# Two-layer trunk on one core: the scan's table copies and the second half's first operands placed behind the loop over channel tiles

## The chip, the cores and the metric

The kernel runs on one core of a Trainium2 chip. The metric is the device time of one execution in microseconds (us); a measurement gives the median of several runs. The engines are named as the profile names them: PE (TensorE, matmul), PEld (its weight loads), DVE (VectorE), ACT (ScalarE), POOL (GpSimd) and SP (SyncE, which issues the DMAs).

## The reference

Two layers of a trunk are computed for two groups of tokens that share their weights: 128 context tokens and 512 tokens that are being denoised, each of width 1024, held together as 640 columns. The part that matters here is the beginning of a layer:

```
mod = silu(c) @ w_ada[l] + b_ada[l]
sh1, sc1, g1, sh2, sc2, g2 = split(mod, 6)
u = x * (1.0 + sc1) + sh1
z = u @ w_in
q, k, v, s_in, f_in, gates = split(z)
...
ssm_y, ssm_state = s5_bidirectional(s_in, a_re, a_im, log_dt, b_re, b_im, c_re, c_im, d, h0)
```

The modulation `mod` comes from the condition vector alone. `u` is the modulated input and the operand of the large product `z`, of which `s_in` feeds a bidirectional state-space scan. The scan's coefficients (powers of exp(a dt), and from them the zero-order-hold input matrices) are computed on the chip from `a_re`, `a_im` and `log_dt`. Attention, a Fourier branch, gating, the output product, a layer norm and a convolution-gated MLP follow; the change does not touch them.

## The kernel before

The 640 columns are worked on in two halves: half 0 has 256 columns (the 128 context tokens and 128 others), half 1 has 384. The 1024 channels are eight tiles of 128, numbered `dt` or `kt`. Products run in split precision: a number is stored as a rounded part h (a cast on ACT, line 113) and the remainder l (a subtraction, line 114, on DVE unless another engine is named), and each tile of a product takes three matmuls, h·h, h·l and l·h (lines 131 to 133, or 1359 in the first loop).

The program begins in `run` (line 1318 on). `silu_c` makes the condition's operand `cs`. `ssm_scalars` (line 463 on) computes, on DVE, the powers `PW` of the scan's coefficient and the table `FB`; eight copies on ACT (lines 568, 569, 571 and 572) then bring them into the layouts `LT` and `FTab`, in one go for both layers (`G` = 64 groups) and separately for the forward partitions 0 to 63 and the backward ones 64 to 127, with the order of the eight time steps turned round in one of the two. The copy writes with the time step as the fastest index of its target and reads with the group as the fastest of its source. Line 573 adds a table with the sign turned.

`ada_first` (line 238) is the first loop: for each of the eight channel tiles it loads a block `ablk` of 1 MB, makes scale and shift of that tile (`adps` on PE, copied to `adar` on ACT, turned round on PE as `adpt`, added up on DVE as `mod`) and calls `block(dt)`. `block` makes the operands of the input product for that channel tile with `modsplit` (line 366): it scales and shifts the input `xs` into a buffer `ut` (two buffers, line 369), on ACT or, for the tiles listed in `MOD0`, on POOL; then it casts `ut` into `uh` on ACT and subtracts into `ul` on DVE. Half 0 is made tile by tile in the loop. Half 1 is made for tiles 0 to 5 when `dt` is `XB` = 5, and tile by tile after that; `MOD0` gives POOL the tiles 1, 3, 5 and 7 of half 1.

While the loop runs, PE already works on the first four weight tiles of the input product for half 0. `WAT` = (3, 6, 7, 7) says at which `dt` each of the four is loaded and begun, with all channel tiles up to there; every later `dt` adds its three matmuls to each open tile. The four sums stay in four PSUM banks (`mm_first`) until the copy `sre` on ACT (line 776) empties them. The products of half 1 over the same tiles (`mm_wz`, lines 131 to 133) take the next bank that comes free.

After the loop, `ssm_prep(0, ...)` makes the scan's matrices for layer 0, eight chunks of them, on DVE and POOL by turns (its first instruction is `nci`, line 617; `pt`, `bb`, `wbt`, `pb` and `wct` are its tiles; it reads `FTab` and `LT`), with transposes (`ptp`) and small products (`pkp`) on PE; and `shift` subtracts the mean of the input (`shs`, `mm_shift`, `xs`). Both are held behind the last subtraction of either half by `behind` (line 95), which lets a scheduler place instructions only after a given one. The layer's scan reads tables (`wbd`, `pd`) that prep has written through DMAs; `Ms` is loaded from `pd`.

The order of instructions on each engine is not written by hand: a scheduler sets it when the program is built, from the order of the code, `behind` and its own estimates. Each engine then works its list off in order, and a waiting instruction holds all behind it.

## Time and profile before

| what | us |
|---|---|
| median of 3 runs | 2289.36 |
| the runs | 2283.41, 2289.46, 2289.36 |
| the profiled execution's own time | 2281.54 |
| its span in the trace | 2279.4 |

The profile shows one execution. Busy time of an engine is the union of its instructions' durations; a row of the timeline gives the start, the duration (of all instructions merged into it) and, in brackets, the idle time of the engine ahead of it and what ended it. Windows give the busy time of each engine in a stretch, the TensorE clock that was granted (1.00 is 2.4 GHz, 0.50 is 1.2 GHz), the share of the DMA engines and the rate of transfers.

### The profile page before, as it was taken

To read this page: it belongs to the slowest core of one execution; us is meant where nothing else is said; L and a number is where in the kernel's file an instruction comes from. 1 tells how busy PE (TensorE), PEld (TensorE's weight loads), DVE (VectorE), ACT (ScalarE), POOL (GpSimd) and SP (SyncE) were. 2 spreads that over 40 slices of the span, in tenths; PEclk is the share of its full clock that TensorE was granted. 3 is DMA by queue.
4 is the path that set the end of the run, shared out by engine and by line. 5 is a ranking of instruction groups with operands and counts; after the bars stand their busy time and mean duration, and the time that the engine had idled before them with its cause. 6 is when DMAs were issued, how large, how long until landed. Compare 5 with 4: busy or idle time off the path is not lost.

```text
span 2279.4 us, 40654 instructions
## 1 busy us (share of the span) xinstructions
PE 2201.7 (97%) x15696; PEld 2114.2 (93%) x15696; DVE 1517.7 (67%) x3638; ACT 879.0 (39%) x1799; POOL 598.5 (26%) x589
## 2 busy tenths in 40 slices
PE   6899999999999999999998999999999999999997
PEld 5889989898799999999998999999879999999997
DVE  7956750466757788999974277357755776475475
ACT  5343232344633441431444322334553443242243
POOL 0439952007354300000035000002535520000003
PEclk8999989999999999999999999999999999999998
DMA  7786575625032135445436745542204122222221
GB/s 277 215 259 213 205 214 168 213 89 165 2 128 82 58 110 167 140 142 184 146 93 174 178 130 146 159 158 78 76 2 153 57 82 67 84 75 65 84 75 47
DMA packets 172641, 293.97 MB, mean 129 GB/s; under 512 B 48128, under 2 KB 114080, under 8 KB 171424
## 3 DMA queue, kind: packets, MB, share of 16 engines
q1 hardware_dynamic: 171584, 291.12, 41.8%
q8 instruction: 124, 2.03, 0.4%
q14 instruction: 69, 0.57, 0.1%
q10 hardware_dynamic: 864, 0.26, 0.1%
HBM read 241.57 MB, written 49.75 MB: 128 GB/s over the span
## 4 chain that ended last, share of the span: by engine, by line
PE 78%; DVE 10%; DMA 6%; ACT 2%; POOL 2%; issue 1%; SPq 1%; POOLq 0%; DVEq 0%; ACTq 0%
PE mm_w_up L133 7%; PE mm_w_up L131 7%; PE mm_w_up L132 7%; PE mm_wz L131 6%; PE mm_wz L132 6%; PE mm_wz L133 6%; PE mm_qkv L1108 4%; PE mm_w_down L131 4%; PE mm_w_down L133 4%; PE mm_w_down L132 4%; DVE adjunk L283 2%; PE mm_pv L1173 2%; PE pt L1226 2%; PE S L1215 2%; PE mm_w_br L131 2%; PE mm_w_br L132 2%
## 5 line engine op out<-in xcount | busy, mean ns | idle before, releaser
L113 ACT CAST wh<-wraw 128x1024 fp32r<-128x1024 f32 (+1 forms) x224 | 232.7, 1039 | 426.4 <-PE mm_w_down L132 118.6
L132 PE MATMUL mm_w_up<-ul,wh 128*128 128x256 f32 (+1 forms) x1280 | 393.9, 309 | 0.0
L133 PE MATMUL mm_w_up<-uh,wl 128*128 128x256 f32 (+1 forms) x1280 | 393.4, 309 | 0.2 <-POOL wl L114 0.2
L131 PE MATMUL mm_w_up<-uh,wh 128*128 128x256 f32 (+1 forms) x1280 | 392.3, 309 | 1.2 <-ACT wh L113 0.8
L114 POOL TENSOR_TENSOR wl<-wraw,wh 128x1024 fp32r<-128x1024 f32 x64 | 157.0, 2454 | 871.6 <-ACT wh L113 854.0
L114 DVE TENSOR_TENSOR wl<-wraw,wh 128x1024 fp32r<-128x1024 f32 (+1 forms) x160 | 203.4, 1271 | 148.7 <-ACT wh L113 146.0
L131 PE MATMUL mm_wz<-uh,wh 128*128 128x384 f32 (+1 forms) x832 | 264.9, 319 | 6.2 <-ACT uh L113 3.2
L1252 DVE SCALAR_TENSOR_TENSOR acc<-mm_w_up,cw,acc 128x127 f32<-128x127 f32 (+2 forms) x616 | 228.5, 398 | 53.9 <-ACT acc L1258 32.7
L132 PE MATMUL mm_wz<-ul,wh 128*128 128x384 f32 (+1 forms) x832 | 261.7, 315 | 2.7 <-DVE ul L114 2.7
L133 PE MATMUL mm_wz<-uh,wl 128*128 128x384 f32 (+1 forms) x832 | 261.8, 315 | 0.0
L131 PEld LDWEIGHTS mm_w_up<-uh,wh 128*128 128x128 f32 x1280 | 241.9, 189 | 1.6 <-ACT wh L113 1.0
L133 PEld LDWEIGHTS mm_w_up<-uh,wl 128*128 128x128 f32 x1280 | 242.2, 189 | 0.6 <-POOL wl L114 0.5
L132 PEld LDWEIGHTS mm_w_up<-ul,wh 128*128 128x128 f32 x1280 | 242.3, 189 | 0.3
L133 PE MATMUL mm_w_down<-hh,wl 128*128 128x256 f32 (+1 forms) x632 | 195.0, 310 | 0.9 <-DVE wl L114 0.9
L132 PE MATMUL mm_w_down<-hh,wh 128*128 128x384 f32 (+1 forms) x632 | 195.5, 310 | 0.0
L131 PE MATMUL mm_w_down<-hh,wh 128*128 128x384 f32 (+1 forms) x632 | 193.5, 311 | 0.0
L131 PEld LDWEIGHTS mm_wz<-uh,wh 128*128 128x128 f32 x832 | 159.2, 191 | 15.0 <-issue 6.3
L132 PEld LDWEIGHTS mm_wz<-ul,wh 128*128 128x128 f32 x832 | 159.4, 192 | 3.8 <-DVE ul L114 3.0
L133 PEld LDWEIGHTS mm_wz<-uh,wl 128*128 128x128 f32 x832 | 159.4, 192 | 1.0 <-issue 1.0
L283 DVE SCALAR_TENSOR_TENSOR adjunk<-araw,cb 128x512 f32<-128x512 f32 x192 | 140.6, 732 | 12.1 <-DMA araw<-in_w_ada_t_dram 8.9
L1258 ACT ACTIVATE acc<-mm_w_up,cw 128x256 f32<-128x256 f32 (+1 forms) x176 | 107.4, 613 | 54.8 <-PE mm_w_up L133 53.3
L133 PEld LDWEIGHTS mm_w_down<-hh,wl 128*128 128x128 f32 x632 | 119.1, 189 | 1.5 <-DVE wl L114 1.5
(464 smaller groups left out, 5257.0 us busy)
## 6 DMA issues: line engine op xcount, KB each, us to landing
wraw<-in_w_up_dram SPq DMA_DIRECT2D x88, 512.0 KB, 3.5
wraw<-in_wz_dram SPq DMA_DIRECT2D x64, 512.0 KB, 3.9
araw<-in_w_ada_t_dram SPq DMA_DIRECT2D x48, 512.0 KB, 3.7
araw<-in_w_ada_dram SPq DMA_DIRECT2D x32, 512.0 KB, 4.2
wraw<-in_w_down_dram SPq DMA_DIRECT2D x32, 512.0 KB, 3.5
wraw<-in_w_br_dram SPq DMA_DIRECT2D x24, 512.0 KB, 3.7
td<-gt SPq DMA_DIRECT2D x48, 192.0 KB, 2.2
tl<-td SPq DMA_DIRECT2D x48, 192.0 KB, 3.4
```

What stands on the lines that cost most here:

```text
L113: nc.scalar.copy(h, src)
L114: return (eng or nc.vector).tensor_tensor(l, src, h.bitcast(F32), OP.subtract)
L131: mm(ps, wh, xh, start=j == 0, stop=False)
L132: mm(ps, wh, xl, start=False, stop=False)
L133: mm(ps, wl, xh, start=False, stop=j == n - 1)
L283: nc.vector.scalar_tensor_tensor(junk[:, :k.stop - k.start], raw[:, d], 1.0, cb[v], OP.mult, OP.mult, accum_out=part[:, c, vec - a, dt + d ...
L1108: nc.tensor.matmul(ps[:, :256], lt, w[:, c0:c0 + 256], start=k == 0, stop=k == 23)
L1173: nc.tensor.matmul(po[64 * hh:64 * hh + 64, :256], vt[:, kt + 1, kv * 64:kv * 64 + 64], PT[hh][:, kt], start=kt == 0, stop=kt == 5, tile_p ...
L1215: nc.tensor.matmul(S[:, b, :384], q, kt[:, hl, P + b * 384:P + (b + 1) * 384], start=hl == 0, stop=hl == 1)
L1226: nc.tensor.transpose(pt[:, j * P:(j + 1) * P], p[:, (3 * b + j) * P:(3 * b + j + 1) * P], self.ident)
L1252: nc.vector.scalar_tensor_tensor(o, src, w, o, OP.mult, OP.add)
L1258: nc.scalar.activation(acc, ps, AF.Identity, bias=b, scale=w1)
```

## The change

The eight copies of the tables leave `ssm_scalars` and become a function `ssm_tables(l)` of its own, called once for each layer after the loop, behind the last cast of half 0 (`cast0`): sixteen copies, each for the 32 groups of one layer. The sign copy is made for each layer, too. The pool `zoh` that holds `PW` and `FB` stays open until then. Half 1's operands are no longer made in the loop at `dt` 5, 6 and 7 but all eight tiles after the last `dt`, and POOL scales all eight (`MOD0`). `WAT` begins the second of the four first weight tiles at `dt` 5 and the third at 6.

```diff
-WAT = (3, 6, 7, 7)
-MOD0 = (((), ()), ((1, 3, 5, 7), ()))
+WAT = (3, 5, 6, 7)
+MOD0 = (((), ()), (range(8), ()))
...
     def split(self, h, l, src, eng=None):
         nc = self.nc
-        nc.scalar.copy(h, src)
+        self.cast = nc.scalar.copy(h, src)
...
-            fw, bw = slice(0, 64), slice(64, 128)
-            for ri in range(2):
-                o = self.LT[:, ri].rearrange("p g t -> p t g")
-                cp = nc.scalar.copy
-                cp(o[fw], PW[fw, ri, 1:9])
-                cp(o[bw, ::-1], PW[bw, ri, 1:9])
-                o = self.FT[:, ri].rearrange("p g t -> p t g")
-                cp(o[fw, ::-1], FB[fw, ri])
-                cp(o[bw], FB[bw, ri])
-            V.tensor_scalar(self.LT[:, 2], self.LT[:, 1], -1.0, None, op0=OP.mult)
...
+            self.powers = PW, FB
+
+    def ssm_tables(self, l):
+
+        PW, FB = self.powers
+        cp = self.nc.scalar.copy
+        gs = slice(32 * l, 32 * l + 32)
+        fw, bw = slice(0, 64), slice(64, 128)
+        for ri in range(2):
+            o = self.LT[:, ri, gs].rearrange("p g t -> p t g")
+            cp(o[fw], PW[fw, ri, 1:9, gs])
+            cp(o[bw, ::-1], PW[bw, ri, 1:9, gs])
+            o = self.FT[:, ri, gs].rearrange("p g t -> p t g")
+            cp(o[fw, ::-1], FB[fw, ri, :, gs])
+            cp(o[bw], FB[bw, ri, :, gs])
+        self.nc.vector.tensor_scalar(self.LT[:, 2, gs], self.LT[:, 1, gs], -1.0, None, op0=OP.mult)
...
-            for half in range(2):
-                if half == 0 or dt > XB:
-                    ends[half] = self.modsplit(xs[half][:, dt], half, sc, sh, dt, self.u[half, "h"], self.u[half, "l"])
+            ends[0] = self.modsplit(xs[0][:, dt], 0, sc, sh, dt, self.u[0, "h"], self.u[0, "l"])
+            self.cast0 = self.cast
             if dt == XB:
                 self.ld(xs[1], self.i["xt"][:, :, HS[1]])
-                for d in range(dt + 1):
-                    ends[1] = self.modsplit(xs[1][:, d], 1, sc, sh, d, self.u[1, "h"], self.u[1, "l"])
...
+            if dt == KT - 1:
+                for d in range(KT):
+                    ends[1] = self.modsplit(xs[1][:, d], 1, sc, sh, d, self.u[1, "h"], self.u[1, "l"])
...
+        with self.behind(self.cast0):
+            for l in range(NL):
+                self.ssm_tables(l)
+        self.zoh.close()
```

What the scheduler makes of it stands in the built programs. ScalarE before, at the end of the loop; `uh_260` is the rounded operand of half 0 and `uh_262` that of half 1, and `ut` with 128x128 are scales of half 0, with 128x384 of half 1:

```order
L113 CAST uh_262<-ut 128x384 x2
L375 ACTIVATE ut<-xs,mod_85,su_264 128x128 x2
L375 ACTIVATE ut<-xs,mod_85,su_264 128x384
L113 CAST uh_260<-ut 128x256
L113 CAST uh_262<-ut 128x384
L375 ACTIVATE ut<-xs,mod_85,su_264 128x128 x2
L113 CAST uh_260<-ut 128x256
L113 CAST uh_262<-ut 128x384
L776 COPY sre<-mm_first 128x256 x3
```

Work on the two halves alternates here, and the table copies are not among these rows: they stand further ahead in the list. ScalarE now, at the same place (`uh_250` is half 0, `uh_252` half 1):

```order
L375 ACTIVATE ut<-xs,mod_85,su_254 128x128 x2
L113 CAST uh_250<-ut 128x256
L375 ACTIVATE ut<-xs,mod_85,su_254 128x128 x2
L113 CAST uh_252<-ut 128x384
L113 CAST uh_250<-ut 128x256
L583 COPY LT<-PW 64x8x32
L584 COPY LT<-PW 64x8x32
L586 COPY FTab<-FB 64x8x32
```

After the last cast of half 0, with one cast of half 1 just ahead of it, the table copies begin. They end, sixteen of them, with this piece of the same list:

```order
L586 COPY FTab<-FB 64x8x32
L587 COPY FTab<-FB 64x8x32
L113 CAST uh_252<-ut 128x384
L785 COPY sre<-mm_first 128x256
L113 CAST uh_252<-ut 128x384
L785 COPY sre<-mm_first 128x256 x2
L113 CAST uh_252<-ut 128x384 x5
L113 CAST wh<-wraw 128x1024
```

Seven casts of half 1 stand behind the sixteen copies, and so does the first copy that empties a bank of the first four weight tiles. VectorE before, where preparation begins (`ul_261` is the remainder of half 0, `ul_263` of half 1):

```order
L114 TENSOR_TENSOR ul_261<-ut,uh_260 128x256
L114 TENSOR_TENSOR ul_263<-ut,uh_262 128x384
L114 TENSOR_TENSOR ul_261<-ut,uh_260 128x256
L114 TENSOR_TENSOR ul_263<-ut,uh_262 128x384
L617 TENSOR_SCALAR nci<-bc 128x64
L625 TENSOR_TENSOR pt_704<-fzero,bc 128x64
```

Preparation follows the last subtraction of the two halves. VectorE now, at the same place:

```order
L114 TENSOR_TENSOR ul_253<-ut,uh_252 128x384
L114 TENSOR_TENSOR ul_251<-ut,uh_250 128x256
L588 TENSOR_SCALAR LT<-LT 128x256 x2
L114 TENSOR_TENSOR ul_253<-ut,uh_252 128x384 x7
L626 TENSOR_SCALAR nci<-bc 128x64
L634 TENSOR_TENSOR pt_713<-fzero,bc 128x64
```

Seven subtractions of half 1 and the two sign copies now stand between the last subtraction of half 0 and preparation.

## Rows read from the trace of the kernel before

**Rows 1.** The page: span, and busy time, share and instructions of each engine.
```profile
span 2279.4 us, 40654 instructions
...
PE 2201.7 (97%) x15696; PEld 2114.2 (93%) x15696; DVE 1517.7 (67%) x3638; ACT 879.0 (39%) x1799; POOL 598.5 (26%) x589
```

**Rows 2.** Windows of 5 us: stretch, length, busy by engine, granted clock, DMA share, GB/s.
```profile
30.00:35.00 5.00, 0.48 (x1) 0.28 (x1) 3.67 (x17) 4.95 (x7) 0.00 (x0) 0.66 1.01 413
35.00:40.00 5.00, 3.55 (x38) 2.61 (x37) 2.14 (x3) 4.97 (x8) 0.00 (x0) 0.50 0.66 223
40.00:45.00 5.00, 4.75 (x28) 4.27 (x31) 2.36 (x5) 4.91 (x9) 1.32 (x2) 0.50 0.40 122
45.00:50.00 5.00, 5.00 (x65) 4.79 (x58) 4.39 (x16) 3.31 (x8) 1.07 (x1) 0.98 0.49 153
50.00:55.00 5.00, 4.05 (x30) 3.44 (x28) 3.03 (x12) 4.33 (x12) 0.66 (x1) 1.00 0.17 63
```

**Rows 3.** Groups by form, ACT, 0 to 130 us: busy us, mean ns | idle before.
```profile
L113 ACT CAST uh<-ut 128x384 fp32r<-128x384 f32 x8 | 4.1, 512 | 1.7 <-POOL ut L373 1.6
L113 ACT CAST uh<-ut 128x256 fp32r<-128x256 f32 x8 | 3.2, 402 | 0.2
...
L375 ACT ACTIVATE ut<-xs,mod,su 128x384 f32<-128x384 f32 x4 | 2.8, 700 | 0.1
L572 ACT COPY FTab<-FB 64x512 f32<-64x512 f32 x2 | 2.3, 1142 | 0.0
...
L569 ACT COPY LT<-PW 64x512 f32<-64x512 f32 x2 | 2.2, 1110 | 0.0
...
L689 ACT COPY Vst<-psv 64x256 f32<-64x256 f32 x2 | 0.7, 363 | 1.0 <-PE psv L685 1.0
```

**Rows 4.** Timeline of ACT: first and last of eight table copies, the loop's last casts.
```profile
28.76 1.13 ACT L568 COPY LT<-PW 64x512 f32<-64x512 f32 x1
...
40.46 1.14 ACT L572 COPY FTab<-FB 64x512 f32<-64x512 f32 x1
...
52.74 0.99 ACT L113 CAST uh<-ut 128x256 fp32r<-128x256 f32 x2
```

**Rows 5.** Timeline of DVE, 48 to 55 us: subtractions of half 1, preparation's start.
```profile
48.00 0.55 DVE L114 TENSOR_TENSOR ul<-ut,uh 128x384 fp32r<-128x384 f32 x1
...
53.76 0.56 DVE L114 TENSOR_TENSOR ul<-ut,uh 128x384 fp32r<-128x384 f32 x1 [0.16 <-ACT uh L113]
54.23 0.19 DVE L617 TENSOR_SCALAR nci<-bc 128x64 f32<-128x64 f32 x1
```

**Rows 6.** Timeline of PE: the first products of half 1.
```profile
55.19 0.44 PE L131 MATMUL mm_wz<-uh,wh 128*128 128x384 f32 x1 [0.30 <-ACT sre L776]
55.47 0.34 PE L132 MATMUL mm_wz<-ul,wh 128*128 128x384 f32 x1
55.64 0.34 PE L133 MATMUL mm_wz<-uh,wl 128*128 128x384 f32 x1
```

**Rows 7.** Windows after the loop, columns as in rows 2.
```profile
55.00:75.00 20.00, 17.77 (x126) 16.21 (x127) 20.00 (x43) 5.23 (x11) 0.52 (x2) 1.00 0.61 158
75.00:105.00 30.00, 24.98 (x209) 22.67 (x208) 29.02 (x52) 9.84 (x22) 22.47 (x25) 1.00 0.80 256
105.00:125.00 20.00, 15.84 (x123) 15.10 (x122) 10.62 (x20) 5.08 (x13) 0.53 (x2) 0.88 1.15 218
125.00:285.00 160.00, 160.00 (x1358) 149.70 (x1357) 113.86 (x295) 58.23 (x143) 131.00 (x170) 0.99 0.67 224
```

**Rows 8.** Timeline of POOL: two of its four scales of half 1.
```profile
43.41 0.66 POOL L373 TENSOR_SCALAR ut<-xs,su,mod 128x384 f32<-128x384 f32 x1 [1.95 <-DVE ul L114]
48.04 1.07 POOL L373 TENSOR_SCALAR ut<-xs,su,mod 128x384 f32<-128x384 f32 x1 [3.98 <-DVE mod L257]
```

**Rows 9.** Waits of PE, 55 to 130 us: total, times, longest.
```profile
PE psv L685 <- DMA Ms<-pd: 4.2, 1, 4.2
```

More of the change, by code (lines that the diff above doesn't have):

```diff
@@ L470, in ssm_scalars @@
         L8 = self.L8 = s.tile([P, 2, G, 2], F32, name="L8")
-        with tc.tile_pool(name="zoh", bufs=1) as z:
+        self.zoh = ExitStack()
+        if True:
+            z = self.zoh.enter_context(tc.tile_pool(name="zoh", bufs=1))
             def t(n):
```

## The prediction

> **What bounds the kernel now.** I read the page first, for the shares: TensorE is busy 97% of the span, VectorE 67%, ScalarE 39% [rows 1]. So most of the span is bound by TensorE, and an edit pays only where TensorE waits. The edit sits in the first 60 us, so the second view is the busy time in stretches of 5 us there [rows 2]. From 30 to 55 us TensorE is busy 0.48 + 3.55 + 4.75 + 5.00 + 4.05 = 17.8 of 25, that is 7.2 idle, 4.5 of them in the first stretch. ScalarE is busy 4.95, 4.97 and 4.91 of 5 from 30 to 45: it is the engine that the loop over channel tiles (dt) waits for. The granted clock falls to 0.66 and 0.50, the 1.2 GHz level, in and after the stretch in which TensorE stood still, and is back at 2.4 GHz after 45.
>
> The third view says what ScalarE does there: its instructions by form [rows 3] and in order of time [rows 4]. The eight table copies take 1.11 to 1.14 us each, eight times about 1.13 or 9.1 us, between 28.8 and 41.6, in the middle of the loop. The loop's last cast of half 0 starts at 52.74 and, at 0.41, ends at 53.15; VectorE subtracts the last tile of half 1 from 53.76 and begins the scan's preparation (nci) at 54.23 [rows 5]; TensorE begins its first product of half 1 at 55.19, held to the last 0.30 by ScalarE's copy that empties a PSUM bank [rows 6].
>
> The fourth view is what follows [rows 7]. From 55 to 105 us VectorE is busy 49.0 of 50: preparation and shift run there without a hole, and TensorE waits for them. From 55 to 125 TensorE is idle 2.2 + 5.0 + 4.2 = 11.4 of 70. From 125 to 285 it is busy 160.00 of 160: a delay that is still there at 125 goes through to the end.
>
> **The change part by part.** The built order shows what the diff only suggests. On ScalarE the eight copies become sixteen of half the size, and all sixteen stand behind the loop's last cast but ahead of seven of the eight casts of half 1. On VectorE seven subtractions of half 1 stand in a row behind the table's sign copy, and nci behind them. On TensorE the first product of half 1 follows the last product of the loop directly, so nothing fills a wait there.
>
> Taking out of the loop: the eight copies (9.1 us of ScalarE), half 1's four scales there (4 x 0.70 = 2.8) and seven of its casts (7 x 0.51 = 3.6) [rows 3]. How much earlier the loop ends is no row's to say. It gains nothing at worst, if loads and TensorE's order pace it: the transfers run at 413 GB/s until 35 us, and TensorE is full from 40 to 50 [rows 2]. At best it gains the 7.2 us that TensorE is idle in it. I take half, 3.5: the idle time of 30 to 35 sits where loads and VectorE, still busy 3.67 of 5, pace the loop too, and only the later part is ScalarE's alone. The loop's last cast then ends at 53.15 - 3.5 = 49.65.
>
> Sixteen copies ahead of half 1: no row has this form. Contiguous casts take 0.40 for 256 elements and 0.51 for 384, so 0.11 for 128 more and 0.18 to start. The copies of 512 elements take 1.13, so 0.95 above the start; half of it is 0.47, and a copy of 256 comes to 0.65. The low bound is the nearest other row of 256 elements on 64 partitions, the Vst copy at 0.36 [rows 3]: 16 x 0.36 = 5.8. The high bound would be 1.14 each if size did not matter, but the two casts exclude that. I take 0.65, from the row with the same strided writing, 16 x 0.65 = 10.4: they end at 60.05. [...]
>
> Half 1's rounds: each tile is scaled by GpSimd in 0.66 [rows 8], cast in 0.51 [rows 3], subtracted in 0.56 [rows 5], and there are two buffers for the scaled tile. A buffer's round is 1.73 us, so one tile follows the other by 0.86. Tile 0 is cast inside the loop and two tiles wait ready when the copies end. Tile 1 is through at 60.05 + 0.51 + 0.56 = 61.1, the other six 6 x 0.86 = 5.2 later, at 66.3. Nci then starts at 66.3 instead of 54.23: **+12.1 on VectorE's chain**. Before, most of these rounds lay inside the loop and their cover was its waiting; now only the first has cover.
>
> TensorE: it needs the bank copy behind the cast of tile 1, so it starts at about 60.05 + 0.41 + 0.4 = 60.9 instead of 55.19, and its three last products need the last subtraction, so the first 24 products end at 66.8. Before they took 24 x 0.17 [rows 6] from 55.19, to 59.3: **+7.5 on TensorE**. It stands still for some nine microseconds ahead of them, and in rows 2 the stretch with 4.5 idle was followed by ten microseconds at 1.2 GHz, so the next 24 products may take 8.2 instead of 4.1: up to +11.6.
>
> GpSimd is idle there otherwise, so its eight scales cost only what they lengthen a round. One of the four scales took 1.07, not 0.66 [rows 8], and it ran from 48.04 while VectorE subtracted from 48.00 [rows 5]: if all six did, 0.41 / 2 x 6 = 1.2 more. I leave that for the high end. [...]
>
> The tiles' due order (the second first tile at dt 5 instead of 6) changes which products fill TensorE inside the loop and no amount of work; I cost it at nothing, inside the 3.5.
>
> **Sum.** At 125 us the delay lies between TensorE's 7.5 and VectorE's 12.1. Since TensorE waits for VectorE's chain in that stretch, and its idle 11.4 us hide only what is not on that chain, I take the middle, +10. The preparation's DMAs move with it: the wait of TensorE for the table Ms, 4.2 us, is already the largest there [rows 9], and it comes from the same chain. The profiled execution took 2281.54 us (span 2279.4); +10 makes 2291.5. That execution lay 7.8 below the median of the runs, 2289.36, so the median that I forecast is 2289.4 + 10 = **2299 us**. Unknown costs at their ends: gain 7.2 and copies at 0.36 put the last copy at 51.7, nci at 58.0 (+3.8) and TensorE's first 24 at 58.5 (-0.8), about +1; gain 0 puts nci at 69.8 (+15.6), with GpSimd's 1.2 about +17. So 2290 to 2306.
>
> **Rivals.** Measurement tells about 0.3% from no change, 6.9 us.
> - *Late operands, as summed* (+7 to +13): 2299. For it: three engines' orders agree, and VectorE is full right after. Chance 0.52.
> - *More, by the lower clock and GpSimd's blocked scales* (+13 to +17): 2304. For it: the fall in rows 2 and the 1.07 in rows 8. Chance 0.13.
> - *Cheap copies.* If the half-size copies cost 0.40 like a contiguous cast, the last ends 4.0 earlier, at 56.05: 2295, which is within 0.3%. Against it: all eight copies of the trace lie between 1.11 and 1.14. Chance 0.10. [...]
> - *Absorbed* (+1 to +5): TensorE's 11.4 idle microseconds from 55 to 125 take the delay, because the transfers that it waits for come by another order of the queue: 2292, within 0.3%. Against it: VectorE has no idle time to give. Chance 0.14.
> - *Faster.* ScalarE alone paces the loop, and without its 9.1 us of copies the clock never falls; the loop's last cast ends at 44.05, copies at 0.36 end at 49.8, TensorE starts half 1 at 50.6 instead of 55.19 (-4.6), and with the queue's other order the 4.2 us wait for Ms goes too: -9, 2280. It decides only if the copies end before 54.23 - 6.3 = 47.9 or VectorE's chain is not what TensorE waits for; for it speaks ScalarE's full 30 to 45 [rows 2], against it the loads until after 35 and TensorE's own full stretch. Chance 0.11.
> - That the scheduler would lift the copies back into the loop is excluded by the built order.
>
> **How the numbers follow.** Faster by over 0.3%: 0.11. Within it: 0.10 + 0.14 = 0.24. Slower: 0.52 + 0.13 = 0.65. The range from 2288 to 2306 takes in the ends +1 and +17 and 2 us of spread below, and leaves out the faster case and little else.
>
> **What would show it.** In the changed profile: sixteen LT and FTab copies near 0.65 us, the first near 50; a hole of 8 to 10 us on TensorE ahead of the first mm_wz product, ended by ScalarE, and a granted clock of 0.50 after it; nci at 66; TensorE full again from about 135. Wrong would be copies of 0.4 or less, a loop that ends before 45, or nci later by 12 while the products at 300 us are late by less than 5.

## The result, and the profile after

| | median, us | range | runs | ratio to before, 95% interval |
|---|---|---|---|---|
| before, same chip | 2289.36 | 2277.22 to 2289.57 | 7 | |
| changed | 2302.77 | 2294.43 to 2309.56 | 7 | 1.0076 (1.0057 to 1.0095) |
| changed, measured again | 2301.81 | 2296.18 to 2310.72 | 6 | 1.0081 (1.0051 to 1.0112) |

The change makes the kernel slower, by about 0.8%, or 17 to 19 us: that is the ratios times 2284, since the kernel before has medians of 2283.3 to 2285.0 in six later measurements of 11 to 25 runs each. Its 2289.36 here is high, and the two medians of this table lie only 13.4 apart. The forecast was slower by 10. The profiled execution took 2309.56 us, the slowest of the seven; its page begins (answering to [rows 1]):

```profile
span 2307.8 us, 40659 instructions
...
PE 2212.0 (96%) x15696; PEld 2119.9 (92%) x15696; DVE 1529.0 (66%) x3639; ACT 879.7 (38%) x1803; POOL 604.7 (26%) x593
```

**The first 70 us.** The timeline of ScalarE, to be read against [rows 4]:

```profile
47.65 0.80 ACT L113 CAST uh<-ut 128x384 fp32r<-128x384 f32 x2
48.35 0.67 ACT L583 COPY LT<-PW 64x256 f32<-64x256 f32 x1
...
58.36 0.65 ACT L587 COPY FTab<-FB 64x256 f32<-64x256 f32 x1
59.03 0.51 ACT L113 CAST uh<-ut 128x384 fp32r<-128x384 f32 x1
59.45 0.37 ACT L785 COPY sre<-mm_first 128x256 f32<-128x256 f32 x1
59.71 0.51 ACT L113 CAST uh<-ut 128x384 fp32r<-128x384 f32 x1
60.12 0.65 ACT L785 COPY sre<-mm_first 128x256 f32<-128x256 f32 x2
```

Sixteen copies of 0.64 to 0.69 us stand between the loop's last cast and everything else: half 1's second cast at 59.03, and the first copy that empties a bank (`sre`) at 59.45. VectorE and TensorE, against [rows 5, 6]:

```profile
66.48 0.56 DVE L114 TENSOR_TENSOR ul<-ut,uh 128x384 fp32r<-128x384 f32 x1 [1.11 <-ACT uh L113]
66.96 0.19 DVE L626 TENSOR_SCALAR nci<-bc 128x64 f32<-128x64 f32 x1
```

```profile
50.05 0.28 PE L1365 MATMUL mm_first<-uh,wl 128*128 128x256 f32 x1
60.82 0.69 PE L131 MATMUL mm_wz<-uh,wh 128*128 128x384 f32 x1 [10.49 <-ACT sre L785]
...
67.41 0.34 PE L133 MATMUL mm_wz<-uh,wl 128*128 128x384 f32 x1
```

TensorE finishes the loop 4.5 us earlier than before (its last `mm_first` product started at 54.6) and then stands still for 10.49 us until the first bank is empty. The 24th product starts at 67.41; the preparation (`nci`) begins 12.7 later than before.

**From 125 us on.** Here before had 160.00 busy of 160 [rows 7]. Windows of the changed kernel:

```profile
105.00:125.00 20.00, 19.55 (x178) 18.66 (x177) 17.21 (x32) 8.07 (x19) 5.45 (x9) 1.00 1.13 176
125.00:145.00 20.00, 18.77 (x150) 18.44 (x151) 9.64 (x17) 7.75 (x25) 6.84 (x10) 0.91 0.99 327
145.00:165.00 20.00, 16.87 (x96) 14.62 (x94) 13.75 (x19) 6.92 (x22) 9.42 (x12) 0.75 0.58 177
...
205.00:285.00 80.00, 76.94 (x635) 71.57 (x634) 68.12 (x184) 23.87 (x48) 72.06 (x97) 0.98 0.60 199
...
345.00:405.00 60.00, 56.11 (x405) 52.26 (x405) 7.32 (x12) 18.93 (x34) 16.97 (x10) 0.97 0.60 189
```

TensorE now waits in three places where it had not waited, and the clock falls to 0.75 in the mean from 145 to 165. The waits, in its timeline:

```profile
155.97 1.14 PE L694 MATMUL psv<-U,wbs 128*128 128x80 f32 x4 [3.13 <-ACT Vst L701]
...
219.58 0.39 PE L133 MATMUL mm_wz<-uh,wl 128*128 128x256 f32 x1 [3.06 <-DVE wl L114]
...
366.45 0.43 PE L131 MATMUL mm_wz<-uh,wh 128*128 128x256 f32 x1 [3.89 <-ACT wh L113]
```

A table of times along the way shows where the loss arises. The last row but one is TensorE's idle time from 0 to 145 us, the last that from 145 us to the first product of the branches (`mm_w_br`), where the input product ends. "Again" is another profiled execution of the same kernel, taken in a later measurement; bc4 is an experiment below.

| us | before | again | changed | again | changed, bc4 |
|---|---|---|---|---|---|
| first transposed product (`ptp`) | 60.3 | 60.5 | 73.4 | 73.4 | 73.1 |
| scan's first step (`scb`) | 186.0 | 187.6 | 200.1 | 200.2 | 193.3 |
| scan's last output (`Yh`) | 323.9 | 322.5 | 345.6 | 341.7 | 330.1 |
| first `mm_w_br` | 411.2 | 408.8 | 433.8 | 430.4 | 415.5 |
| end | 2279.4 | 2281.2 | 2307.8 | 2304.1 | 2288.6 |
| PE idle to 145 | 32.2 | 32.7 | 37.5 | 37.6 | 38.5 |
| PE idle, 145 to `mm_w_br` | 3.5 | 2.6 | 14.1 | 10.7 | 6.6 |

From the first `mm_w_br` to the end all five take 1868 to 1874 us. So nearly all of the loss is made before 434 us: some 5 us of idle time up to 145; by a lower clock there 4 to 6 (the granted clock from 0 to 145 is 0.89 in the mean instead of 0.92 to 0.93, times 145 us); 7 to 12 us of idle time after 145, where the forecast had expected none; and by a lower clock there 3 to 9 more (0.96 instead of 0.97 to 0.99 from 145 to `mm_w_br`). The terms overlap, since the clock is also below 1.00 in some of the stretches where TensorE stands still (0.61 in the mean from 50.33 to 60.82 and 0.85 from 152.84 to 155.97 in the changed kernel, though 1.00 in the holes that end at 219.58 and 366.45), so their sum is more than the 19 to 25 us by which `mm_w_br` is late. These executions lie 23 to 28 us apart at the end, more than the medians: those of the changed kernel took 6.8 and 4.1 us more than the medians of their runs.

### The profile page after: what moved, and what is told of

The parts are those of the page before. It is cut to its first block, busy times and chain, and to the rows that moved or that the text cites. A ratio compares the mean times of both kernels' runs of the same rounds, so it can differ in the third digit from the quotient of the medians.

```text
span 2307.8 us, 40659 instructions
## 1 busy us (share of the span) xinstructions
PE 2212.0 (96%) x15696; PEld 2119.9 (92%) x15696; DVE 1529.0 (66%) x3639; ACT 879.7 (38%) x1803; POOL 604.7 (26%) x593
## 4 chain that ended last, share of the span: by engine, by line
PE 81%; DVE 7%; DMA 5%; POOL 2%; ACT 2%; SPq 1%; issue 1%; POOLq 0%; ACTq 0%; DVEq 0%
PE mm_w_up L133 8%; PE mm_w_up L131 8%; PE mm_w_up L132 8%; PE mm_wz L131 5%; PE mm_wz L132 5%; PE mm_wz L133 5%; PE mm_w_down L131 4%; PE mm_w_down L133 4%; PE mm_w_down L132 4%; PE mm_qkv L1117 4%; PE mm_pv L1182 2%; PE pt L1235 2%; PE S L1224 2%; PE mm_w_br L131 2%; PE mm_w_br L132 2%; PE mm_w_br L133 2%
## 5 line engine op out<-in xcount | busy, mean ns | idle before, releaser
L113 ACT CAST wh<-wraw 128x1024 fp32r<-128x1024 f32 (+1 forms) x224 | 232.8, 1040 | 426.7 <-PE mm_w_down L132 118.3
L114 DVE TENSOR_TENSOR wl<-wraw,wh 128x1024 fp32r<-128x1024 f32 (+1 forms) x160 | 214.1, 1338 | 141.3 <-ACT wh L113 140.7
L131 PE MATMUL mm_wz<-uh,wh 128*128 128x384 f32 (+1 forms) x832 | 267.0, 322 | 20.0 <-ACT sre L785 11.8
L1261 DVE SCALAR_TENSOR_TENSOR acc<-mm_w_up,cw,acc 128x127 f32<-128x127 f32 (+2 forms) x616 | 228.9, 399 | 53.8 <-ACT acc L1267 32.7
L131 PEld LDWEIGHTS mm_wz<-uh,wh 128*128 128x128 f32 x832 | 161.8, 195 | 28.1 <-ACT sre L785 12.3
L283 DVE SCALAR_TENSOR_TENSOR adjunk<-araw,cb 128x512 f32<-128x512 f32 x192 | 141.0, 734 | 13.7 <-DMA araw<-in_w_ada_t_dram 10.4
```

Of the source, the lines that this page charges most:

```text
L113: self.cast = nc.scalar.copy(h, src)
L114: return (eng or nc.vector).tensor_tensor(l, src, h.bitcast(F32), OP.subtract)
L131: mm(ps, wh, xh, start=j == 0, stop=False)
L283: nc.vector.scalar_tensor_tensor(junk[:, :k.stop - k.start], raw[:, d], 1.0, cb[v], OP.mult, OP.mult, accum_out=part[:, c, vec - a, dt + d ...
L1261: nc.vector.scalar_tensor_tensor(o, src, w, o, OP.mult, OP.add)
```

## The experiments

The theory at the start: the copies stand ahead of half 1's operands, and that delay goes through. The rivals: GpSimd's scaling of the whole half; and work of GpSimd and VectorE that falls together during the scan. Every ratio is to the kernel before, run beside it on the same chip.

**1. The copies behind half 1's casts.**

```diff
-        with self.behind(self.cast0):
+        with self.behind(self.cast):
```

> The changed kernel with the sixteen table copies put behind half 1's last cast instead of behind the loop's last cast; all else as in the change. Theory (the copies delay half 1's operands): half 1's casts now run from about 48.4 us at 0.9 to 1.2 each, so they end near 56 us instead of 66.5, TensorE's 24th product of the second half comes near 57 us (67.4 in the changed kernel, 59.3 before), and nearly all of the loss is gone: ratio to before 0.998 to 1.003. Rival 1 (GpSimd's scaling of the whole half is what costs): ratio stays 1.004 or more, although the copies are out of the way. Rival 2 (the loss after 125 us comes from how GpSimd's and VectorE's instructions fall together during the scan, not from the size of the delay): ratio anywhere from 1.000 to 1.006, with a VectorE subtraction of over 5 us in the trace wherever it is high.

Measured: 1.0046 (1.0028 to 1.0064). The theory missed. Half 1 starts at 51.08, but the copies now stand ahead of the next eviction, and TensorE waits as long as in the changed kernel, only later:

```profile
68.84 0.69 PE L131 MATMUL mm_wz<-uh,wh 128*128 128x384 f32 x1 [10.90 <-ACT sre L785]
```

The trace also has the sign of rival 2, a subtraction of VectorE of 11.13 us at 204.02.

**2. The copies alone.** `modsplit` of half 1 goes back into the loop, `WAT` and `MOD0` are those of before, and the copies stand behind the loop's last cast.

> Only the copies move: sixteen of them, by layers, behind the loop's last cast, which is now half 1's last; half 1 is cast in the loop with the scaling shared as before. Theory (the copies cost what they stand in front of): half 1's casts are not delayed but end some 4 to 7 us earlier than before (near 47 us), nothing of half 1 waits, and the 10.4 us of copies stand in front of the evictions of the first products and of the preparation's products with the tables; first product of half 1 at 48 to 52 us (55.2 before), the eviction delay gives some of it back: ratio 0.998 to 1.003. Rival 1 (any 10 us of copies behind the loop costs its 10 us, whatever is queued behind it): ratio 1.004 to 1.006.

Measured: 1.0066 (1.0043 to 1.0089), outside the theory. VectorE begins the preparation 5.2 us *earlier* than before, TensorE waits all the same, for the eviction alone:

```profile
48.99 0.19 DVE L626 TENSOR_SCALAR nci<-bc 128x64 f32<-128x64 f32 x1
```

```profile
60.11 0.69 PE L131 MATMUL mm_wz<-uh,wh 128*128 128x384 f32 x1 [10.47 <-ACT sre L785]
```

Up to 145 us TensorE is idle 31.1 us, less than before's 32.2; from there to `mm_w_br` 12.3 against 3.5. In this execution the whole loss lies behind 145 us.

**3. Half 1 alone.** The kernel before with half 1's casts behind the loop, GpSimd's scaling and the new `WAT`; the copies stay in the loop.

> Only half 1 moves: behind the loop and scaled by GpSimd alone, first operands at 3, 5, 6, 7; the table copies stay inside the loop in their eight whole pieces, as before. Theory (copies in front): the loop is shorter by half 1's casts and scalings (about 5 us of ScalarE), half 1 follows at about 47 us with 0.9 to 1.2 us per tile, its last cast near 55 us, so the first 24 products end within 2 us of before's 59.3: ratio 0.998 to 1.002. Rival 1 (GpSimd's scaling is what costs): ratio 1.004 or more.

Measured: 1.0086 (1.0055 to 1.0116). No copies are in the way, and TensorE starts half 1 at 54.08, 1.1 us earlier than before, but half 1's rounds end late (`nci` in the row, 54.23 before), and the loss is as large as with everything:

```profile
60.18 0.19 DVE L617 TENSOR_SCALAR nci<-bc 128x64 f32<-128x64 f32 x1
```

**4. Half 1 scaled by both engines.** `MOD0` of before in the changed kernel.

> The changed kernel with half 1's scaling shared as before (GpSimd the odd tiles, ScalarE the even ones); copies and casts stay where the change puts them. Theory (copies in front): the copies still stand ahead of the casts; ScalarE adds four scalings of 0.70 us (2.8 us) but waits less for GpSimd (three waits of 1.16 and one of 0.53 in the changed kernel's trace, 4.0 us), so the end of half 1's casts moves by less than 2 us and the ratio stays within 0.003 of the changed kernel's 1.0076. Rival 1 (GpSimd's scaling is what costs): ratio 1.004 or less.

Measured: 1.0058 (1.0039 to 1.0078), within the theory's range; `nci` comes at 66.4 instead of 67.0. GpSimd's scaling costs at most a small part: the ratio is 0.0018 lower without it, within the two intervals. After four runs: neither part is free, their losses do not add, and the loss is not read from the first products. Two rivals remain, long instructions of VectorE beside GpSimd (theory A) and the late start of the preparation (theory B).

**5 and 6. GpSimd beside the scan.** In the changed kernel's trace one subtraction of VectorE took 10.59 us instead of 1.23, and GpSimd had no hole from 205 us until 218.45, a microsecond before that subtraction's end:

```profile
208.94 10.59 DVE L114 TENSOR_TENSOR wl<-wraw,wh 128x1024 fp32r<-128x1024 f32 x1 [2.65 <-ACT wh L113]
```

```profile
208.27 1.30 POOL L652 TENSOR_TENSOR wbt<-wbt,pb 128x512 f32<-128x512 f32 x1
209.52 0.34 POOL L636 TENSOR_TENSOR bb<-pt,bb 128x64 f32<-128x64 f32 x1
...
217.38 1.07 POOL L651 TENSOR_TENSOR pb<-bc,FTab 128x512 f32<-128x512 f32 x1
```

Both kernels get the edit that moves such subtractions to GpSimd:

```diff
-PZ = (range(24, 32), range(8))
+PZ = (range(12, 32), range(8))
```

> The changed kernel with the subtractions (wl) of the weight units 12 to 31 of layer 0's first product on GpSimd instead of 24 to 31, so that during the scan no VectorE instruction with both operands in SBUF but the copies Hr stands beside GpSimd's run. In the traces so far one such instruction took 9 to 12 us (10.59 in the changed kernel at 208.9 us) while GpSimd worked back to back. Theory A (such a starved instruction is the surplus over the local delay): no VectorE instruction of over 5 us before 285 us, spread of the runs under 8 us (15 in the changed kernel), and the ratio to the kernel before lower than 1.0076 by 0.003 to 0.006. Theory B (the surplus is only the late start of the preparation, carried to the products that wait for the scan): ratio stays at 1.006 to 1.009.

> The kernel before with the same one edit (weight units 12 to 31 subtracted on GpSimd). The trace of before shows no subtraction over 2.1 us in the scan, so theory A expects 0.997 to 1.001 here, and a distance to the changed kernel with the same edit of 0.003 to 0.004 (7 to 9 us, the local delay alone). Theory B expects the distance to stay at 0.006 to 0.009, whatever this ratio is.

Measured: 1.0055 (1.0035 to 1.0075) and 1.0018 (1.0001 to 1.0035): the distance is 0.0037, but the changed kernel gained only 0.0021 and its runs still spread over 16 us. No instruction of VectorE is over 5 us before 345 us in either. But the edit also shortens the scan (84.9 us from its first to its last step instead of 99.7), so it doesn't isolate the long subtraction. Inconclusive between the two theories.

**7. The copies on GpSimd, in the loop** of the kernel before.

```diff
-                cp = nc.scalar.copy
+                cp = nc.gpsimd.tensor_copy
```

> The kernel before with its eight table copies on GpSimd, which stood idle until 43 us, instead of ScalarE; nothing is behind the loop. Taking the copies out of ScalarE's loop ended the last first product at 50.1 us in the changed kernel instead of 54.6. Theory (what the change gains is this 4.5 us, what it loses is that the 10.4 us of copies stand ahead of the first evictions on ScalarE): first product of half 1 at 50 to 52 us (55.2), no wait of 10 us on TensorE, ratio 0.997 to 1.000. Rival (GpSimd's copies run slower than 1.5 us each, or hold VectorE's instructions that build the tables): GpSimd's scalings of half 1 come after 43 us, and the ratio is 1.000 to 1.004.

Measured: 1.0013 (0.9995 to 1.0031), as the rival said: eight copies took 1.22 to 2.17 us until 42.8, a scaling of half 1 after them 2.02, and half 1's first product came at 57.58, later than before's 55.19.

**8. Eight copies behind the loop.** Layer 1's were to follow `shift`; in the built order layer 0's went into the loop and layer 1's took the place behind it.

> The changed kernel with only layer 0's eight copies behind the loop; layer 1's eight follow the last subtraction of the shift, near 98 us. In the changed kernel TensorE waited 10.49 us (50.3 to 60.8) for the eviction of its first product, which stood behind the sixteen copies. Theory (TensorE waits for as many copies as stand ahead of the first eviction): with eight of 0.65 us the wait is 5.2 us, first product of half 1 near 55.5 us, and the ratio falls by 0.002 to 0.003 to 1.005. (The order built for it puts some or all of layer 0's copies into the loop again: then the wait is as long as the copies that remain ahead of the eviction.) Rival (the start of the preparation alone decides, not TensorE's wait): ratio follows the start of the preparation's products, 67 us in the changed kernel and 54 before.

Measured: 1.0084 (1.0052 to 1.0116). TensorE's wait is the price of the copies ahead of the eviction, half as many and half as long, as expected:

```profile
55.11 0.69 PE L131 MATMUL mm_wz<-uh,wh 128*128 128x384 f32 x1 [4.83 <-ACT sre L785]
```

And the time did not follow it: 5.7 us won at the first product, nothing at the end. That is a sign that the end hangs on something later. In the profiled execution `mm_w_br` comes at 422.0, 11.8 earlier than in the changed kernel's, but the rest takes 1878.1 us (1877.9 in experiment 3), 4 more than the longest of the table: part of the loss of these two arises behind `mm_w_br`, and no experiment shows why.

**9. Layer 1's copies out of the way.** The kernel before, tables by layers; layer 0's in the loop, layer 1's behind a ScalarE copy (`wtt`) of the preparation's second chunk.

> The kernel before with only layer 1's eight copies moved: the tables are copied by layers, layer 0's eight in the loop, layer 1's eight on ScalarE behind the second chunk's transposed copies of the preparation (near 80 us), where ScalarE is busy a third of the time and neither a first eviction nor a cast of half 1 is queued behind them. Half 1 stays in the loop as before. Theory (what stands directly behind the copies on ScalarE sets their price): the loop is shorter by the copies taken out of it (8 of 0.65 us, of which 0 to 4.5 us show), no wait of over 2 us on TensorE between 50 and 70 us, ratio 0.997 to 1.000. Rival (ScalarE's copies are hidden in the loop and cost the preparation when they come later): ratio 1.001 to 1.004.

Measured: 1.0012 (0.9993 to 1.0030). Half 1 starts at 53.22 (55.19 before) and TensorE has no wait of over 2 us from 50 to 70. But the 2 us won at 55 us are not there at the end. The eight copies run from 77.25 to 82.59, and directly behind them in ScalarE's list stands the copy `bz`, which the preparation's products need; TensorE waits for it for 4.79 us, until 83.30, almost as long as for the eight copies of experiment 8.

**10 and 11. Both kernels once more.**

> The changed kernel once more, with a profile of another execution. Theory A (a starved VectorE instruction is the surplus over the local delay, and comes in some executions only): if the trace shows none of over 5 us before 345 us, the time is near the lower end of its runs (2294 to 2300); if it shows one, 2300 or more. The local part is the same each time: TensorE waits 10.4 to 10.6 us for its first eviction and the first negated table operand (nci) comes at 66 to 67 us. Theory B (the surplus is carried by the late start alone): the time lies anywhere in 2294 to 2310, whether or not such an instruction is there.

> The kernel before against itself: ratio 1.000 within its interval, which tells what these intervals are worth. Its trace: no VectorE instruction of over 5 us before 345 us if the time is below 2285 (theory A); products, evictions and casts up to 60 us at the same times as in the first trace, within 1.5 us.

Measured: 1.0081 (1.0051 to 1.0112) and 0.9991 (0.9975 to 1.0006), the latter telling what these intervals are worth. The changed kernel's profiled execution took 2305.91 us and had no VectorE instruction over 5 us before 345 us, so theory A falls as the main cause. Its windows, against those of the changed kernel above:

```profile
145.00:165.00 20.00, 16.95 (x97) 14.70 (x96) 13.88 (x20) 7.25 (x22) 9.68 (x12) 0.75 0.60 176
...
205.00:285.00 80.00, 80.00 (x672) 73.78 (x670) 61.12 (x195) 26.38 (x54) 79.41 (x103) 1.00 0.62 208
...
345.00:405.00 60.00, 55.63 (x396) 51.68 (x395) 6.83 (x11) 18.24 (x32) 13.08 (x7) 0.97 0.59 189
```

The hole of 3.06 from 205 to 285 is gone with the long subtraction, and `mm_w_br` comes 3.4 us earlier: that is about its price. The holes near 155 and 363 are the same in both: they belong to the changed kernel.

**12 and 13. The preparation's inputs.** What makes the hole at 155? The scan's product there waits for the chain of the preparation, and in it GpSimd had waited for its inputs `bc`:

```profile
138.16 0.29 POOL L634 TENSOR_TENSOR pt<-fzero,bc 128x64 f32<-128x64 f32 x1 [13.24 <-DMA bc<-in_ssm_bc_dram]
```

This wait is not made by the change. The kernel before has it too, as long and 11.8 us earlier, and neither the rows nor the prediction name it:

```profile
126.37 0.29 POOL L625 TENSOR_TENSOR pt<-fzero,bc 128x64 f32<-128x64 f32 x1 [13.60 <-DMA bc<-in_ssm_bc_dram]
```

There are two buffers for `bc`, so a chunk's load is queued late, and SP's queue issues it behind other transfers, those of `Ms` (which need a stored `pd`) among them; in the kernel before, too, a load of `bc` at 132.08 stands right behind six of `Ms`. SP's timeline of the changed kernel:

```profile
120.06 5.82 SPq L103 DMA_DIRECT2D Ms<-pd  x6
...
131.62 0.46 SPq L103 DMA_DIRECT2D bc<-in_ssm_bc_dram  x1
...
140.89 1.85 SPq L103 DMA_DIRECT2D Ms<-pd  x4
142.84 0.37 SPq L103 DMA_DIRECT2D bc<-in_ssm_bc_dram  x1
```

Four buffers let each load go two chunks earlier:

```diff
-            bc = z.tile([P, 4, 4, 16], F32, name="bc", tag="bc", bufs=2)
+            bc = z.tile([P, 4, 4, 16], F32, name="bc", tag="bc", bufs=4)
```

> The changed kernel with four buffers instead of two for the preparation's inputs (bc), so that each chunk's load is issued two chunks earlier on SP's queue and no longer stands right behind the loads of Ms, which wait for a store of pd to land. In both traces of the changed kernel GpSimd waited 13.2 and 13.5 us for bc (to 138 us) and VectorE 2 us (to 147 us), and TensorE then 3.1 us for the scan's first products (psv, to 156 us), followed by 10.2 us at half clock. Theory C (the late preparation meets SP's queue there, and this and the waits that follow from a late scan are the surplus of 15 us): these waits go, psv's wait and the half clock behind it with them (7 us), and the scan starts 5 to 10 us earlier; ratio to the kernel before 1.003 to 1.005. Theory B' (the preparation's own work, 113 us from its first to its last transposed product in every kernel, sets the scan's start, and its inputs are never what is late): ratio stays at 1.006 to 1.009.

> The kernel before with four buffers for bc. Its trace shows no wait of TensorE from 125 to 285 us, so there is little to gain: theory C expects 0.998 to 1.000, and so a distance to the changed kernel with the same edit of 0.003 to 0.006, which is the local delay of 6 to 7 us and what of it remains; theory B' expects the distance to stay at 0.006 to 0.009.

Measured: **1.0023** (1.0003 to 1.0042) for the changed kernel, 1.0003 (0.9987 to 1.0019) for the one before. This one edit takes 0.0053 to 0.0058 of the loss away, 12 to 13 of 17 to 19 us, and none of it from the kernel before. The windows of the changed kernel with it:

```profile
145.00:165.00 20.00, 19.90 (x169) 18.82 (x168) 16.57 (x33) 9.13 (x29) 7.98 (x13) 1.00 0.85 269
...
205.00:285.00 80.00, 80.00 (x651) 74.71 (x644) 65.85 (x204) 26.26 (x53) 78.72 (x99) 1.00 0.61 204
...
345.00:405.00 60.00, 60.00 (x418) 55.84 (x417) 8.58 (x13) 18.87 (x34) 11.94 (x5) 1.00 0.58 187
```

The wait for the eviction is still there (10.5 us), `ptp` still starts at 73.1; but the scan starts 7 us earlier, and the holes near 155 and 363 are gone. The before kernel's scan starts 11 to 12 us earlier with the edit (175.4), and the kernel's time does not move: there TensorE had no such hole to close. So the edit shortens the preparation in both kernels, and that pays only where TensorE waits for it. Theory C is half right: the waits behind a late scan are most of the surplus, but the preparation does not meet SP's queue because it is late, since before meets it as well.

The edit also lets the scheduler set another order, on TensorE from some 135 us on. The product that waited at 155.97 keeps its place in TensorE's list, though: 988 products stand ahead of it in the changed kernel and 985 with four buffers, where it starts at 154.8 without a wait. So this hole was closed by the earlier chain and not by a later place in the list; for the hole at 363 that is not shown.

**14 and 15. The copies alone and half 1 alone, once more,** one profiled execution each.

> Copies alone once more, another execution. Its first profile was the fastest of six (2290 of 2290 to 2305 us) and had a starved VectorE copy of 11.9 us at 275.6 us, which TensorE waited for 6.3 us. Theory A (such starvation makes the slow executions): a slow execution shows more or longer ones. Theory C (waits that a late scan makes): up to 145 us the trace is that of the first look, and what a slow execution has more are waits of TensorE of 1 to 6 us for psv, psy or weights, each followed by half clock.

> Half 1 alone once more, another execution (first profile 2303 us of 2288 to 2315, a starved subtraction of 9.1 us at 191 us). Theory A: if this one is near 2288 it has no starved instruction; if near 2310, one or more. Theory C: the local part (first table operand nci at 60 us, six later than before) is the same, and the time follows the sum of TensorE's waits and half-clock stretches between 105 and 430 us.

Measured: 2303.84 us (the first profiled execution took 2290.38) and 2297.33 (2303.44). The copies alone showed three long instructions of VectorE this time, one at 11.93 in the first execution:

```profile
199.45 10.30 DVE L114 TENSOR_TENSOR wl<-wraw,wh 128x1024 fp32r<-128x1024 f32 x1 [2.00 <-ACT wh L113]
...
281.30 6.77 DVE L728 COPY Hr<-Vst 64x512 f32<-64x512 f32 x1
288.08 5.24 DVE L730 COPY Hr<-Vst 64x512 f32<-64x512 f32 x1
```

With them `mm_w_br` came at 426.7 instead of 421.5, which is 5.2 of the 13.5 us; the other 8.3 arise behind `mm_w_br`. Half 1 alone had one such subtraction both times (9.14 and 9.31), 6 us apart in time. So these instructions are part of the spread and not all of it. In the copies alone they are also most of TensorE's idle time behind 145 us: 10.5 of 12.3 us in the first execution and 8.9 of 13.8 in the second are waits for `Hr` or `wl` of VectorE.

**16 to 18. Does anything beat both?** Experiment 9 with four buffers; four buffers with the `PZ` of experiment 5; all three.

> The kernel before with layer 1's eight copies behind the second chunk of the preparation (2.2 us earlier first products when it ran alone) and four buffers for bc together. Theory C (a local gain is kept if the preparation's inputs are not late and nothing new stands on TensorE's path): first product of half 1 at 53.2 us as in the run with the layer 1 copies alone, scan no later than 186 us, ratio 0.997 to 1.000. Rival (what happens up to 105 us hardly counts for the end, since the scan's chain and the rows of waits behind it decide): ratio 1.000 to 1.003, although the first products are 2 us earlier.

> The kernel before with four buffers for bc and weight units 12 to 31 subtracted on GpSimd. Alone, the first started the scan at 175 us (187 before), the second made it 84 us long (94). Theory C (TensorE has no wait in the scan's stretch of the kernel before, so an earlier end of the scan gains only the two waits of psy and the half clock behind them, 6 to 10 us by the traces of before): ratio 0.996 to 1.000. Rival (GpSimd becomes late with the weights): 1.000 to 1.004, with waits for wl on TensorE.

> The kernel before with all three edits that were near or below 1.000: layer 1's eight copies behind the second chunk of the preparation, four buffers for bc, and weight units 12 to 31 subtracted on GpSimd. If their gains add (0.9989 and 0.9988 with one or two of them, of which bc alone was 1.0003): first product of half 1 at 53.2 us, scan of some 83 us from about 181, ratio 0.996 to 0.999 with an interval below 1. If they only shift the same waits: 0.998 to 1.001.

Measured: 0.9989 (0.9971 to 1.0007), 0.9988 (0.9972 to 1.0004) and 0.9999 (0.9986 to 1.0012). None can be told from the kernel before. The gains don't add: with all three, a row of eight subtractions on VectorE (`gl`), each 0.59 to 0.84 us in the kernel before, took 14.55 us from 321.35 on, and GpSimd worked without a hole from 314 to 335 us; with this order it still had its weights and layer 1's preparation to do there. That this is why they don't add is not shown.

## Why the prediction was wrong

**What held.** The prices of the first 70 us were right. Copies: 0.65 forecast, 0.64 to 0.69 measured. Sixteen of them, 10.4 forecast, 10.7 from 48.35 to 59.01. The first product of half 1: 60.9 forecast, 60.82; and its cause, the bank copy, was named. `nci`: 66.3 forecast, 66.96. The loop ended somewhat earlier than forecast (copies from 48.35 instead of 49.65), and half 1's rounds were slower, 1.16 us per tile instead of 0.86: GpSimd scales two tiles, ScalarE casts two, VectorE subtracts two, in turns. The two misses nearly cancel. (In the sum for TensorE, 0.41 is the cast of half 0; a cast of half 1 takes 0.51 by rows 3, which makes 0.1 us.)

**What failed** is the step from 125 us to the end: "From 125 to 285 it is busy 160.00 of 160: a delay that is still there at 125 goes through to the end", and with it the +10, the middle between TensorE's 7.5 and the 12.1 of VectorE's chain. A full stretch only says that nothing in it was late by the old times. TensorE works off a fixed list, and in it stand products that need the scan's chain (`psv`, `psy`) and weights whose cast stands behind the scan's output on ScalarE. In the kernel before they cost TensorE 3.5 us of waiting from 145 us on.

In the changed kernel the chain kept its delay, 12.5 to 14 us (73.4 against 60.3 and 60.5, 200.1 against 186.0 and 187.6), and TensorE's own delay went another way. By an estimate from the traces, which counts the columns that its products have put through, TensorE reaches what before had done at 100 us 8.9 later, at 125 us 6.7 later (7.1 in the second execution) and at 145 us 5.9 (6.2): less than the forecast's +10. Then it meets the chain. Behind the hole at 155.97, at what before had done at 165 us, it is 13.6 late (13.7), as late as the chain; behind the hole at 366.45, at before's 365 us, it is 22.7 late (19.2), of which the long subtraction of the first execution made a part. Behind each hole stands a stretch at a lower clock: the granted clock is 0.50 from 159 to 165, 0.66 in the mean from 219 to 224 and 0.58 from 366 to 370, where the products of 384 columns start 0.32 us apart (0.17 from 370.09 on). At a granted clock of 0.50 (367 to 369.5), 384 columns in 0.32 us are an estimated 1.2 columns per ns, and this is all that the runs show of the prediction's 1.2 GHz: they give the clock as a share of its full value. With four buffers, which shorten the chain, the same estimate gives 8.9 at 125, 8.5 at 165 and 4.3 at 365. So the delay did not pass through: TensorE's was replaced by the chain's, and grew again where the scan's output stood ahead of weights. Experiment 12 shows that the holes go when the preparation is shorter; 2, 3 and 8 show that what TensorE waits for in the first 70 us has little to do with the loss.

**Luck in the number.** The measured 2302.77 lies inside the range of 2288 to 2306, but the forecast starts from 2289.36, a median that was high. From 2284, as the kernel before measures later, the same +10 gives 2294 and the ends +1 and +17 give 2285 and 2301; the changed kernel's second median is 2301.81. The loss of 17 to 19 us lies at or beyond the forecast's upper end.

**The rivals.** *More, by the lower clock and blocked scales* (+13 to +17, 0.13) came nearest to the loss, for the wrong places: the clock does fall to 0.72 in the mean from 55 to 75, but the surplus is made after 145, and half 1's scaling by GpSimd costs nothing that can be told (experiment 4). Single scales of half 1 took 0.66 us (at 45.84) and 1.08 (at 64.83, beside subtractions of VectorE) in the changed kernel; that such a scale is blocked was the author's reading of the 1.07 in rows 8, and no run shows what lengthens it. *Cheap copies* and *faster* fell with the copies' 0.65 and the 10.49 us wait. *Absorbed* fell too, though TensorE's idle time from 105 to 125 did shrink, from 4.16 us to 0.45: some of the delay was taken up there, and came back later.

**What stays open.** Four buffers for `bc` were not tried with the copies alone or half 1 alone; whether these two lose by a late chain, as the changed kernel does, is not shown, and the waits of the copies alone speak for VectorE's long instructions instead (experiments 14 and 15). Every edit makes the scheduler set a new order, and how much of a ratio is that order alone was not measured. The remaining 0.002 between experiments 12 and 13 is within their intervals; as the forecast's local delay it would be 4.6 us.

## What to carry to other kernels

A copy on an engine that works in order is priced by what is queued directly behind it, evictions of PSUM and operands of the next chain alike: sixteen copies made TensorE wait 10.49, 10.47 and 10.90 us in the three places tried behind the loop, eight of them 4.83 and 4.79. Whether such a wait shows at the end is another question (experiments 2 and 8). A stretch in which the bound engine is full is no proof that a delay passes it unchanged: list what the engine's queue takes in there from other chains, and how much earlier than needed each of them comes. Where one chain is later than the bound engine, do not take the middle of the two delays; look for the place where the engine next needs that chain. And a chain that has become late can be shortened anywhere: a wait of 13 us for inputs stood in both kernels, and two more small buffers, worth nothing in the one (1.0003), took back two thirds of the loss in the other.

## What the runs showed of the hardware

Two executions of the changed kernel, measured apart, agree to a few hundredths of a microsecond in what was read of the first 70 us (60.82 and 60.78 for the first product of half 1, behind a wait of 10.49 in both), and still differ by 3.4 us at `mm_w_br`: what tells these two executions apart is made later.

Some instructions of VectorE with all their operands in SBUF took many times their time while GpSimd worked beside them: subtractions of 1.23 us took 9.14 and 9.31 (half 1 alone, experiments 3 and 15), 10.30 (the copies alone, experiment 14), 10.59 (the changed kernel) and 11.13 (experiment 1), and a copy `Hr` of 0.63 took 11.93 (the copies alone, experiment 2). The subtraction of 10.59 us started at 208.94, when a GpSimd instruction was already running (208.27 to 209.57); it outlasted this one and the twelve that followed without a hole, and ended at 219.53, 1.08 us after the last of them: about its own time, as if it had done all its work once GpSimd had stopped. The one of 10.30 us ended at 209.75, with GpSimd still at work until 209.91, so this is not how all of them end. The scan's steps, which have an operand in PSUM (`scb`), took 0.21 to 0.30 us throughout the changed kernel. Eight other subtractions of this form took 1.22 to 2.24 us there between 225 and 289 us, beside the same kind of GpSimd work. What holds VectorE up at some such moments and not at others no run here shows.
